# The second norm's rows turned by VectorE instead of TensorE, for two of four token blocks

## The chip, the cores and the metric

The kernel runs on one core of a Trainium2 chip. The metric is the device time of one execution in microseconds, the median of several runs. The core has five instruction streams: TensorE (matmuls, "PE" in the profile, with its weight loads as "PEld"), VectorE ("DVE"), ScalarE ("ACT"), GpSimd ("POOL") and SyncE ("SP"), which here only issues transfers. Each runs its own queue in order, and they wait for each other by semaphores.

## What is computed

One layer of a decoder for 2048 tokens of width 1024, in float32. The part that matters here is the second half:

```python
x = x + jnp.concatenate([o_hg, o_rw], axis=-1) @ w_out[l]
x = x + _conv_ffn(_rmsnorm(x, norm2_w[l]), w_up[l], conv_w[l], conv_b[l], w_down[l])
return _rmsnorm(x, final_norm_w)
```

`_rmsnorm` divides each token's row by the root of its mean square and multiplies it by a row of weights. `_conv_ffn` multiplies by `w_up` (1024 x 5632), applies a causal convolution of width 3 along the tokens, a gate with SiLU, and `w_down` (2816 x 1024).

## The kernel before

The tokens are four blocks of 512. All large products are made of three float32r matmuls: each operand is split in a high and a low part (ScalarE casts the high part, VectorE subtracts to get the low part), and high x high, high x low and low x high are summed (`mm3`, L270 to L272). The splits of weights go through rings of five buffers (`uwh`, `uwl`, L254 and L255).

Stage 1 (`phase1`) holds the first norm, the input projection, the two mixers and the output projection of blocks 0 to 2. Its constants lie in the tile `cst`. Stage 2 begins with the output projection of block 3 (L1199 to L1276), which leaves the rows of `x` after the first residual in DRAM, `x1d[b]`, one row a token.

Then comes the up-projection. It needs the normed rows with the features on the partitions: `h2d[b]`, 1024 x 512. For blocks 0 and 1 this was done in stage 1. The up-projection is written as a scheme of seven products (Strassen's, in Winograd's form) over pairs of blocks and halves of the weights: `run()` loops over `n`, 22 column blocks for blocks 0 and 1 and then 22 for blocks 2 and 3; each `n` is seven products (`prod`) of 4 x 3 matmuls of 128x512 into `ua`, `ub` and `ud`. The weights of one `n` are four loads of 256 KB (`uraw`, L1178, a ring of six), the sums of weights are L1389, L1390, L1465 and L1470, and the gated results leave as `gd`, L1497, two stores an `n`.

While blocks 0 and 1 are multiplied, the inputs for blocks 2 and 3 are prepared "aside": after each product, `aside(n)` takes one job from a list. `norm_last(b, i2)` puts in 14 jobs for each group of 256 tokens, four groups in all: a load of two tiles of 128 rows (L1298), a pause, two scalings (`rstd` on ScalarE, then L1301 on VectorE), two pauses, and eight times one step of `transposed`. A step is two transposes of 128x128 on TensorE into a PSUM bank (L264), an eviction on ScalarE that multiplies by the norm's weight of that feature, now one value a partition (L122), and a store of 128 x 256 to `h2d` (L1306). The jobs that follow in the list (`four`, L1315) read `h2d` of blocks 2 and 3 and form sums for the scheme; later ones (`sums`, L1341) form sums for the down-projection.

The tiles `h2`, the squares of `rstd` and all raw rows share one ring of six buffers, `br`. All transfers named here are issued by SP, one after the other. A scheduler that runs when the kernel is built gives the order of each engine's queue: an instruction whose inputs are there earlier can stand ahead of one that the code has before it.

The last stage is the down-projection (`da`, `db`), again seven products, with the last norm and the output.

Of the kernel before, what the change touches and what calls it, by code (L numbers as in the profile page):

```python
# [7 lines left out]
F32 = mybir.dt.float32  # L8
# [3 lines left out]
AF = mybir.ActivationFunctionType  # L12
ALU = mybir.AluOpType
# [5 lines left out]
P = 128  # L19
T = 2048  # L20
D = 1024
KD = D // P
# [45 lines left out]
def tile_layer(ctx, tc, consts, x, norm1_w, w_in, hg_lb_logits, hg_norm_w, rw_shift_mu, rw_w0, rw_w2,  # L68
# [4 lines left out]
    V, S, TE = nc.vector, nc.scalar, nc.tensor  # L73
    dma, store = nc.sync.dma_start, nc.gpsimd.dma_start
# [12 lines left out]
    cst = cp.tile([P, C_ID], F32, name="cst")  # L87
# [11 lines left out]
    def pst(name):  # L99
        return pools["ps"].tile([P, 512], F32, tag="mm", name=name, bufs=8)  # L100
# [13 lines left out]
    def act(out_, in_, func, **kw):  # L114

        want = tables.get(func)
        if want is not None and want != tab["now"]:
            pre = S.preload_act_table_set(want)
            for u_ in tab["uses"]:
                tc.add_manual_dep(pre.ins, u_.ins.name, NOSYNC, reason="table order")  # L120
            tab.update(now=want, pre=pre, uses=[])
        i_ = S.activation(out_, in_, func, **kw)  # L122
        if want is not None:
            tc.add_manual_dep(i_.ins, tab["pre"].ins.name, NOSYNC, reason="table order")
            tab["uses"].append(i_)
        return i_

    def rstd(pool, xt, name, sqt="nsq", sqb=1):

        sq = pool.tile([P, D], BF16, tag=sqt, name="nsq", bufs=sqb)  # L130
        st = pool.tile([P, 2], F32, tag="nst", name=name, bufs=8)
        act(sq, xt, AF.Square, accum_out=st[:, 0:1])
        act(st[:, 1:2], st[:, 0:1], AF.Ln, bias=eps6, scale=1.0 / D)
        act(st[:, 1:2], st[:, 1:2], AF.Exp, scale=-0.5)
        return st[:, 1:2]
# [23 lines left out]
    def vec(nm, i):  # L159
        return vt[:, off[nm] + i:off[nm] + i + 1]  # L160
# [24 lines left out]
    x1d = [dp.tile([BLK, D], F32, name=f"x1d{b}") for b in range(NBLK)]  # L185
    h2d = [dp.tile([D, BLK], F32, name=f"h2d{b}") for b in range(NBLK)]
# [71 lines left out]
    def transposed(xt, nm, psum, evict):  # L258

        n = len(xt)  # L260
        for k in range(KD):
            tp = psum()
            for i in range(n):
                TE.transpose(tp[:, i * P:(i + 1) * P], xt[i][:, k * P:(k + 1) * P], ident)  # L264
            evict(k, tp[:, :n * P], vec(nm, k))
            yield 109 * n
# [879 lines left out]
    with ExitStack() as c2:  # L1146
        wr = c2.enter_context(tc.tile_pool(name="wr2", bufs=1, reuse_waits="tile"))
        hp = c2.enter_context(tc.tile_pool(name="hp2", bufs=1, reuse_waits="tile"))
        hr = c2.enter_context(tc.tile_pool(name="hr2", bufs=1, reuse_waits="tile"))
# [33 lines left out]
        with tc.tile_pool(name="op", bufs=1, reuse_waits="tile") as op_:  # L1183
# [7 lines left out]
            b = NBLK - 1  # L1191
# [41 lines left out]
            def weights(k, dh):  # L1233
                raw = ring("w", w_out[0, k * P:(k + 1) * P, dh * 512:dh * 512 + 512])
                wh, wl = (wo_[c].pop() if wo_[c] else
                          op_.tile([P, 512], F32R, tag="wo" + c, name="wo" + c, bufs=3) for c in "hl")
                split_next(wh, wl, raw)
                return wh, wl

            xt = {}  # L1240
# [4 lines left out]
            for dh in range(2):  # L1245
                accs = [pst("wacc") for _ in range(4)]
                for n, k in enumerate((0, 1, 4, 5, 2, 3, 6, 7)):
                    w = weights(k, dh)
                    if dh == 0:
                        take(k)  # L1250
                    if n == 5:
                        for i in range(4):
                            t0 = b * BLK + i * P
# [10 lines left out]
                    if dh == 1 and 2 <= n:  # L1264
                        for j in range(2):
                            q = 2 * (n - 2) + j
# [3 lines left out]
                    for q in range(12):  # L1270
                        i, t_ = (q % 4, q // 4) if first else (q // 3, q % 3)
# [7 lines left out]
        with tc.tile_pool(name="up", bufs=1, reuse_waits="tile") as up:  # L1279
            Bh[2], Bl[2] = (hp.tile([P, 4, BLK], F32R, tag=f"B{c}2", name=f"B{c}2") for c in "hl")  # L1280
            halo = up.tile([P, 2 * NFF + 52, 2], F32, name="halo")
            V.memset(halo, 0.0)


            side, first_at = [], [1]

            def aside_of(fs):

                side.extend((first_at[0], f) for f in fs)

            def norm_last(b, i2):

                xt = []

                def load():
                    for q in range(2):
                        xt.append(up.tile([P, D], F32, tag="xt2", name="xt2", bufs=2))
                        dma(xt[q], x1d[b][(i2 * 2 + q) * P:(i2 * 2 + q + 1) * P, :])  # L1298

                def scale(q):  # L1300
                    V.tensor_scalar_mul(xt[q], xt[q], rstd(hr, xt[q], "nst", "br", 6))  # L1301

                def evict(k, tp, w):
                    t_ = hr.tile([P, 256], F32, tag="br", name="h2", bufs=6)
                    act(t_, tp, AF.Copy, scale=w)
                    dma(h2d[b][k * P:(k + 1) * P, i2 * 256:i2 * 256 + 256], t_)  # L1306

                g = transposed(xt, "n2", lambda: pst("tp"), evict)
                aside_of([load, None, lambda: scale(0), lambda: scale(1), None, None] + [lambda: next(g)] * KD)

            def four(srcs, make, dsts):

# [15 lines left out]
            for b in (2, 3):  # L1328
                for i2 in range(2):
                    norm_last(b, i2)  # L1330
# [172 lines left out]
    with tc.tile_pool(name="dn", bufs=1, reuse_waits="tile") as dn:  # L1503
# [39 lines left out]
        def evict(g, p, accs, i):  # L1543

            if p in (0, 2, 4):
                add(g, *((0, 0), None, (0, 1), None, (1, 1))[p], i, accs["a"][i])
            if p == 1:
                pend.append(lambda: add(g, 0, 0, i, accs["b"][i]))
            if p == 4:
                pend.append(lambda: add(g, 1, 1, i, accs["b"][i]))  # L1550
            if p == 5:
                pend.append(lambda: (add(g, 1, 0, i, accs["a"][i]), finish(g, 1, i)))
            if p == 6:
                pend.append(lambda: (add(g, 0, 1, i, accs["b"][i]), finish(g, 0, i)))
# [10 lines left out]
        for s_ in range(DS, N):  # L1565
            g, p, kk = steps[s_]
# [60 lines left out]
```

## Time and profile before

| | |
|---|---|
| median of 3 runs | 2648.05 us (2644.51 to 2653.97) |
| the profiled execution | 2645.14 us, its span 2643.1 us |
| mean granted clock of TensorE | 0.992 |
| TensorE busy | 2545.1 us, 96% |
| VectorE busy | 1973.0 us, 75% |
| ScalarE busy | 1356.5 us, 51% |
| GpSimd busy | 381.1 us, 14% |
| moved by the DMA engines | 523.18 MB, 198 GB/s |

The span runs from the first to the last instruction. In the views of the profile a line such as "L1306" is a line of the kernel; "out<-in" names the tiles; "xN" is a count. A group shows its busy time, the mean of one in ns, and the idle time of its engine just before, with what ended it. A window shows the busy time of each engine in it, the clock that TensorE was granted, the mean busy share of the DMA engines and what they moved. A line of waits is "engine and line <- engine and line that ended the wait: total us, times, longest". A line of one source or tile is minimum, median and maximum of the duration in ns, then the first and last start.

### The profile page before, as it was taken

To read this page: it belongs to the slowest core of one execution; us is meant where nothing else is said; L and a number is where in the kernel's file an instruction comes from. 1 tells how busy PE (TensorE), PEld (TensorE's weight loads), DVE (VectorE), ACT (ScalarE), POOL (GpSimd) and SP (SyncE) were. 2 spreads that over 40 slices of the span, in tenths; PEclk is the share of its full clock that TensorE was granted. 3 is DMA by queue.
4 is the path that set the end of the run, shared out by engine and by line. 5 is a ranking of instruction groups with operands and counts; after the bars stand their busy time and mean duration, and the time that the engine had idled before them with its cause. 6 is when DMAs were issued, how large, how long until landed. Compare 5 with 4: busy or idle time off the path is not lost. (4 is left out here: it accounts for less than half of the span.)

```text
span 2643.1 us, 51079 instructions
## 1 busy us (share of the span) xinstructions
PE 2545.1 (96%) x19403; PEld 2044.3 (77%) x19403; DVE 1973.0 (75%) x3760; ACT 1356.5 (51%) x2242; POOL 381.1 (14%) x686
## 2 busy tenths in 40 slices
PE   7999999999999899999899999999999999999998
PEld 5877777767777667777678888787888887888887
DVE  4978576676676765787678799987998887766556
ACT  5565444555445554354466754556554544545444
POOL 6433222212222122232100000000000000000000
PEclk9999999999999999999999999999999999999999
DMA  8847464656665566856574477747764553998665
GB/s 305 243 161 204 141 173 128 149 152 212 191 180 145 168 212 184 262 167 164 188 260 136 129 233 255 230 152 228 245 204 130 169 172 128 337 318 280 204 192 187
DMA packets 415115, 523.18 MB, mean 198 GB/s; under 512 B 149280, under 2 KB 245910, under 8 KB 414870
## 3 DMA queue, kind: packets, MB, share of 16 engines
q1 hardware_dynamic: 360337, 341.59, 41.3%
q0 software_dynamic: 54464, 178.32, 21.1%
q8 instruction: 152, 2.49, 0.4%
q14 instruction: 94, 0.76, 0.1%
q10 hardware_dynamic: 68, 0.02, 0.0%
HBM read 372.99 MB, written 134.22 MB: 192 GB/s over the span
## 5 line engine op out<-in xcount | busy, mean ns | idle before, releaser
L270 PE MATMUL pj<-hh,wh 128*128 128x512 f32 x960 | 392.3, 409 | 4.7 <-ACT rkv L122 2.1
L271 PE MATMUL pj<-hl,wh 128*128 128x512 f32 x960 | 379.1, 395 | 0.0
L272 PE MATMUL pj<-hh,wl 128*128 128x512 f32 x960 | 378.3, 394 | 0.0
L270 PE MATMUL ua<-Bh,uwh 128*128 128x512 f32 x704 | 276.9, 393 | 6.7 <-ACT m L122 5.8
L272 PE MATMUL ua<-Bh,uwl 128*128 128x512 f32 x704 | 274.5, 390 | 0.0
L271 PE MATMUL ua<-Bl,uwh 128*128 128x512 f32 x704 | 274.3, 390 | 0.0
L270 PEld LDWEIGHTS pj<-hh,wh 128*128 128x128 f32 x960 | 181.2, 189 | 53.7 <-issue 9.0
L272 PEld LDWEIGHTS pj<-hh,wl 128*128 128x128 f32 x960 | 181.3, 189 | 39.3 <-issue 0.3
L271 PEld LDWEIGHTS pj<-hl,wh 128*128 128x128 f32 x960 | 181.5, 189 | 35.1 <-issue 0.6
L254 ACT CAST uwh<-uraw 128x512 fp32r<-128x512 f32 x220 | 134.1, 617 | 128.7 <-PE ua L271 54.1
L255 DVE TENSOR_TENSOR dal<-draw,dah 128x512 fp32r<-128x512 f32 x138 | 95.4, 691 | 107.0 <-ACT dah L254 106.7
L255 DVE TENSOR_TENSOR uwl<-uraw,uwh 128x512 fp32r<-128x512 f32 x220 | 147.6, 687 | 33.7 <-ACT uwh L254 33.6
L254 ACT CAST dah<-draw 128x512 fp32r<-128x512 f32 x138 | 85.6, 621 | 159.2 <-PE da L271 74.0
L270 PEld LDWEIGHTS ua<-Bh,uwh 128*128 128x128 f32 x704 | 132.2, 188 | 38.3 <-ACT m L122 10.6
L272 PEld LDWEIGHTS ua<-Bh,uwl 128*128 128x128 f32 x704 | 132.2, 188 | 28.0 <-DVE uwl L255 0.4
L271 PEld LDWEIGHTS ua<-Bl,uwh 128*128 128x128 f32 x704 | 132.3, 188 | 26.7
L270 PE MATMUL ud<-Bh,uwh 128*128 128x512 f32 x352 | 138.1, 392 | 0.0
L1497 POOL DMA_DIRECT2D gd<-y x2 | 1.1, 540 | 947.9 <-DVE y L1495 947.9
L272 PE MATMUL ud<-Bh,uwl 128*128 128x512 f32 x352 | 137.2, 390 | 0.0
L271 PE MATMUL ud<-Bl,uwh 128*128 128x512 f32 x352 | 137.1, 390 | 0.0
L271 PE MATMUL da<-dbl,dah 128*128 128x512 f32 x332 | 129.5, 390 | 0.2 <-DVE dbl L255 0.2
L272 PE MATMUL da<-dbh,dal 128*128 128x512 f32 x332 | 129.3, 389 | 0.0
(581 smaller groups left out, 6191.6 us busy)
## 6 DMA issues: line engine op xcount, KB each, us to landing
uraw<-in_w_up_dram SPq DMA_DIRECT2D x176, 256.0 KB
woraw<-in_w_out_dram POOLq DMA_DIRECT2D x96, 256.0 KB, 3.4
br<-gd SPq DMA_DIRECT2D x88, 256.0 KB
draw<-Sg SPq DMA_DIRECT2D x88, 256.0 KB
draw<-Tw SPq DMA_DIRECT2D x88, 256.0 KB
gd<-y SPq DMA_DIRECT2D x86, 256.0 KB
Sg<-br SPq DMA_DIRECT2D x72, 256.0 KB
xt<-x1d SPq DMA_DIRECT2D x32, 512.0 KB
```

The costliest lines, as they stand in the source:

```text
L254: S.copy(hi, src)
L255: V.tensor_sub(lo, src, hi.bitcast(F32))
L270: TE.matmul(acc, lh, rh, start=first, stop=False, skip_group_check=skip)
L271: TE.matmul(acc, lh, rl, start=False, stop=False, skip_group_check=skip)
L272: TE.matmul(acc, ll, rh, start=False, stop=last, skip_group_check=skip)
L1497: (dma if end is None else nc.gpsimd.dma_start)(gd_[2 * h + b][fb * P:(fb + 1) * P, :], ys[0][:, b * BLK:(b + 1) * BLK])
```

## The change

The eight steps of each `norm_last` group become four "turns" with a pause after each, so the list of jobs keeps its length. VectorE transposes each 32x32 block on its own, so that a block's 32 tokens lie along the free dimension and its 32 features on 32 partitions; the rest of the transposition is in the addresses of the stores. The 256 tokens of a group are loaded so that each quarter of the partitions holds 64 tokens in a row, as two sets of 32 (four loads of 256 KB for two of 512 KB). One turn takes 256 features: one instruction of 128 x 512 elements and four stores, each from 32 partitions, 64 KB in runs of 256 bytes.

The norm's weight is no longer one value a partition at that point. It is multiplied in the scaling, with a row of weights that is the same on all partitions: `n2row`, loaded once, 512 KB, over the first 1024 columns of `cst`, which stage 2 doesn't use.

```diff
             V.memset(halo, 0.0)
+            n2row = cst[:, 0:D]
+            dma(n2row, norm2_w.broadcast_to([P, D]))
...
                 def load():
-                    for q in range(2):
-                        xt.append(up.tile([P, D], F32, tag="xt2", name="xt2", bufs=2))
-                        dma(xt[q], x1d[b][(i2 * 2 + q) * P:(i2 * 2 + q + 1) * P, :])
+                    xt.append(up.tile([P, 2, D], F32, tag="xt2", name="xt2"))
+                    v = x1d[b][i2 * 256:i2 * 256 + 256, :].rearrange("(g q t) d -> g t q d", g=4, q=2)
+                    for g in range(4):
+                        dma(xt[0][32 * g:32 * g + 32], v[g])
 
                 def scale(q):
-                    V.tensor_scalar_mul(xt[q], xt[q], rstd(hr, xt[q], "nst", "br", 6))
-
-                def evict(k, tp, w):
-                    t_ = hr.tile([P, 256], F32, tag="br", name="h2", bufs=6)
-                    act(t_, tp, AF.Copy, scale=w)
-                    dma(h2d[b][k * P:(k + 1) * P, i2 * 256:i2 * 256 + 256], t_)
-
-                g = transposed(xt, "n2", lambda: pst("tp"), evict)
-                aside_of([load, None, lambda: scale(0), lambda: scale(1), None, None] + [lambda: next(g)] * KD)
+                    t_ = xt[0][:, q]
+                    V.scalar_tensor_tensor(t_, t_, rstd(hr, t_, "nst", "br", 6), n2row, ALU.mult, ALU.mult)
+
+                def turn(m):
+                    t_ = hr.tile([P, 8, 2, 32], F32, tag="br", name="h2", bufs=6)
+                    V.transpose(t_.rearrange("p c q t -> p q c t"),
+                                xt[0][:, :, m * 256:m * 256 + 256].rearrange("p q (c t) -> p q c t", t=32))
+                    for g in range(4):
+                        t0 = i2 * 256 + g * 64
+                        dma(h2d[b][m * 256:m * 256 + 256, t0:t0 + 64].rearrange("(c p) t -> p c t", p=32),
+                            t_[32 * g:32 * g + 32].rearrange("p c q t -> p c (q t)"))
+
+                aside_of([load, None, lambda: scale(0), lambda: scale(1), None, None]
+                         + [f for m in range(4) for f in (lambda m=m: turn(m), None)])
```

## The prediction

> **What bounds the kernel now.** I read the page first, then the stage of the change in windows, then its waits.
>
> ```profile
> span 2643.1 us, 51079 instructions
> PE 2545.1 (96%) x19403; PEld 2044.3 (77%) x19403; DVE 1973.0 (75%) x3760; ACT 1356.5 (51%) x2242; POOL 381.1 (14%) x686
> ```
>
> TensorE is busy 96% of the span, so the question is whether it is also what sets the pace where the transposes stand. I cut the second stage at the first `ub` matmul of a pass of the up-projection (one pass is 7 products, 84 matmuls). The first row holds the eight passes in which the norm is done, the second the next five, the third the five after those; the last two are single passes of the first eight.
>
> ```profile
> 1378.80:1539.30 160.50, 160.50 (x737) 131.62 (x736) 126.46 (x194) 109.95 (x182) 0.00 (x0) 1.00 0.40 127
> 1539.30:1634.50 95.20, 95.20 (x422) 78.83 (x421) 92.38 (x145) 47.70 (x70) 0.00 (x0) 1.00 0.80 264
> 1634.50:1733.80 99.30, 96.45 (x423) 78.60 (x422) 91.41 (x147) 48.48 (x72) 0.00 (x0) 1.00 0.72 234
> ...
> 1499.20:1518.70 19.50, 19.50 (x90) 16.06 (x89) 16.56 (x26) 15.54 (x26) 0.00 (x0) 1.00 0.38 126
> 1518.70:1539.30 20.60, 20.60 (x99) 16.87 (x97) 14.89 (x24) 12.16 (x21) 0.00 (x0) 1.00 0.44 136
> ```
>
> Columns: length, then busy time of PE, PEld, DVE, ACT, POOL, granted clock, DMA share, GB/s. In the norm passes TensorE is busy for all of 160.50 us, at full clock, and a pass is longer the more transposes it holds (4 in the 19.50, 12 in the 20.60). The next five passes have none and take 95.20/5 = 19.04 us each, TensorE again without a gap although VectorE is at 92.38/95.20 = 97%. In the third row TensorE does lose 99.30 - 96.45 = 2.85 us. Who waits in the norm passes:
>
> ```profile
> ACT uwh L254 <- PE ua L271: 30.0, 20, 2.0
> DVE uwl L255 <- ACT uwh L254: 20.6, 16, 2.3
> ```
>
> ScalarE waits 30 us for TensorE to give a weight buffer back, and VectorE waits for ScalarE: the makers of the operands run as far ahead as their five buffers allow. TensorE itself is missing from the list of waits here. So this stage is TensorE's, and its own instructions are what counts.
>
> **What is removed.** 64 transposes in 32 pairs, 32 evictions on ScalarE, 32 stores of 128 KB.
>
> ```profile
> L264 PEld LDWEIGHTS tp<-ident,xt x64: 138/139/144, 1395.0 to 1536.4; 128*128 128x128 f32 x64
> L264 PE MATMUL tp<-ident,xt x64: 270/271/275, 1395.2 to 1536.5; 128*128 128x128 f32 x64
> L122 ACT ACTIVATE h<-tp,vt x32: 467/468/472, 1395.7 to 1536.9; 128x256 f32<-128x256 f32 x32
> ```
>
> 64 times 271 ns would be 17.3 us, but matmuls overlap, so the price is read from the starts:
>
> ```profile
> 1394.77 0.39 PE L271 MATMUL ua<-Bl,uwh 128*128 128x512 f32 x1
> 1394.99 0.39 PE L272 MATMUL ua<-Bh,uwl 128*128 128x512 f32 x1
> 1395.22 0.38 PE L264 MATMUL tp<-ident,xt 128*128 128x128 f32 x2
> 1395.36 0.47 PE L270 MATMUL ud<-Bh,uwh 128*128 128x512 f32 x1
> 1395.67 0.39 PE L271 MATMUL ud<-Bl,uwh 128*128 128x512 f32 x1
> ```
>
> From 1394.99 to 1395.67 there are two steps of 0.23 and the pair: 0.68 - 0.46 = 0.22 us a pair, 32 x 0.22 = 7.0 us. The windows give more: 160.50 - 8 x 19.04 = 8.2 us. I take 8.2, since it is the whole difference between passes with and without, and keep 7.0 as the low end. ScalarE loses 15.0 us of evictions; it was waiting there already, so I count nothing.
>
> **What is added to VectorE.** Four turns a group, 16 in all, each 128x512, and the two scalings of a group become a scaling with a row of weights.
>
> ```profile
> L765 DVE STREAM_TRANSPOSE ATb<-AR 128x512 f32<-128x512 f32 x16 | 10.9, 694 | 0.0
> L810 DVE STREAM_TRANSPOSE TZ<-Ti 128x512 f32<-128x512 f32 x8 | 8.5, 1061 | 0.8 <-DMA xt<-in_x_dram 0.2
> L1301 DVE TENSOR_SCALAR xt<-xt,nst 128x1024 f32<-128x1024 f32 x8 | 5.7, 751 | 0.2
> L1490 DVE SCALAR_TENSOR_TENSOR y<-cg,cvt,y 128x1024 f32<-128x1024 f32 x44 | 56.2, 1278 | 0.0
> ```
>
> L765 reads whole runs, L810 reads with a stride. The new turn reads runs of 256 elements and scatters whole 32-element rows, so it is nearest to L765: 16 x 0.694 = 11.1 us (17.0 by L810). The scaling: 8 x (1.278 - 0.751) = 4.2 us. VectorE then has 126.5 + 15.3 = 141.8 us in 8 x 19.04 = 152.3, 93% (97% by L810). The fullest passes are those with two scalings and a turn: 16.56 + 0.69 + 1.05 = 18.3 of 19.04. The five passes of the second row ran at 97% without a loss, so I charge nothing inside the stage. What hides it is the lead; after it come those five passes, which may live on it. If they arrive without it they could lose as the third row does, 2.85/99.3 x 95.2 = 2.7 us. Between 0 and 2.7 I take 0.8, since VectorE still idles 10 us in the stage.
>
> [...]
>
> **What is added to SP's queue.** 64 stores of 64 KB in runs of 256 B instead of 32 of 128 KB in runs of 1 KB, and four loads a group for two.
>
> ```profile
> L1306 SPq DMA_DIRECT2D h2d<-h x32: 319/320/413, 1396.2 to 1537.4; - x32
> L757 SPq DMA_DIRECT2D KBT<-KBb x128: 591/640/3207, 89.0 to 1201.6; - x128
> L1298 SPq DMA_DIRECT2D xt<-x1d x8: 319/376/752, 1367.9 to 1497.7; - x8
> L1178 SPq DMA_DIRECT2D uraw<-in_w_up_dram x172: 367/384/1269, 1365.8 to 2208.7; - x172
> ...
> 716.66 11.37 SPq L757 DMA_DIRECT2D KBT<-KBb  x11
> ...
> 709.74 1.96 SPq L745 DMA_DIRECT2D Ed<-M  x4
> 715.46 1.15 SPq L748 DMA_DIRECT2D E<-Ed  x2
> ```
>
> The nearest issue is L757, 64 KB from 32 partitions in short runs: 0.64 us, or 11.37/11 = 1.03 us each in a row. In one group, two passes of 38.1 us, SP issues 16 such stores, 4 loads, 8 weight loads and 4 stores of the gate: 16 x 0.69 + 16 x 0.45 = 18.2 us with the gaps, 23.7 us at 1.03. SP has room. Behind a store that waits for its turn on VectorE stand the weight loads, and behind those ScalarE's cast. Their slack:
>
> ```profile
> 1436.77 0.39 SPq L1178 DMA_DIRECT2D uraw<-in_w_up_dram  x1
> ...
> 1445.99 0.69 DVE L1389 TENSOR_TENSOR s<-uraw 128x512 f32<-128x512 f32 x1
> ```
>
> 9.2 us from issue to first use, against 4 x 1.03 = 4.1 us for the four stores of a turn. I charge 0. The first row of windows has the DMA engines at 0.40, so bytes are not short either. The reads of the second norm's rows by the next job wait for the same distance of jobs as before, so nothing moves there.
>
> **The row of weights.** One load of 4 KB to each of 128 partitions, 512 KB, into the space of the constants, which have their last reader at 1267.6 us. It has no wait left; where it stands in SP's queue the trace cannot show.
>
> ```profile
> L1006 DVE COPY_PREDICATED A<-cst,hg x80: 217/227/302, 108.8 to 1267.6; 128x64 f32<-128x64 uint32 x80
> ...
> 1300.00:1310.00 10.00, 8.81 (x34) 5.82 (x34) 9.34 (x13) 9.36 (x15) 2.36 (x4) 1.00 0.15 49
> ...
> 1365.00:1370.00 5.00, 3.28 (x14) 2.18 (x12) 4.20 (x8) 4.13 (x8) 0.00 (x0) 1.00 0.88 274
> ...
> 1355.42 2.11 SPq L1276 DMA_DIRECT2D x1d<-xh  x4
> 1357.62 2.74 SPq L1161 DMA_DIRECT2D br<-Ts  x4
> ...
> 1363.36 2.61 ACT L247 CAST Bh<-br 128x512 fp32r<-128x512 f32 x4 [4.33 <-DMA br<-Ts]
> ```
>
> In the code it stands behind the stores L1276. There ScalarE waits 4.33 us for the loads of `Ts`, and TensorE has 3.28 of 5 us: whatever delays those loads is paid by TensorE. 512 KB at 274 GB/s are 1.9 us, and with an issue of 0.38 it is 2.3 us. But SP's queue is not in the order of the code (the loads of L1161 run past L1276), and with no wait the load can slip into a hole such as 1300 to 1310, where the DMA share is 0.15: then it costs 0. I take 1.0.
>
> **The sum.** -8.2 + 0.8 + 0 + 1.0 = -6.4 us against the profiled execution, 2645.14 us (a span of 2643.1 and 2.0 around it): 2638.7. The median of the runs is 2648.05, 2.9 above that execution, so the forecast for the median is 2641.6.
>
> **Rivals.**
>
> *VectorE becomes the bound.* For it: 18.3 of 19.04 us in the fullest passes, in-order behind ScalarE, and 97% if a turn costs what L810 does. Against it: the second row. If the norm passes lose at the third row's rate, 2.9% of 152.3 = 4.4 us, and the next five 2.7: -8.2 + 4.4 + 2.7 + 1.0 = -0.1, 2648.
>
> *The small stores hold SP up (the other side).* Place: SP's queue in the norm passes. The stage is then 4 x (16x + 7.2) us for x us a store. It overtakes TensorE's 38.1 us a group from x = 1.93 and the old stage from x = 2.06. For it: L757 has one of 3.207 us, and four stores to DRAM (Ed, runs of 128 B) had landed only within 715.46 - 709.74 = 5.7 us, 1.43 each. Against it: that is under 1.93, and those stretches carried other traffic; with one row of many for it I give it 0.10. Halfway between 1.43 and 3.2, x = 2.3: 4 x 44.0 = 176.0, +15.5 and 1.0 for the row: 2664.5. [...]
>
> *More is gained.* ScalarE has 15 us less and operands arrive earlier; if the 2.85 us of the third row go too and the row slips into a hole: -8.2 - 2.85 = -11.0, 2637. Against it: VectorE, not ScalarE, is late in that row.
>
> *The change does nothing for the pace.* Only if something else than TensorE paced the norm passes; it has no idle time there, so this gets no chance of its own.
>
> **How the numbers follow.** Forecast 0.60, VectorE's bound 0.16, slow stores 0.10, more gained 0.14. The forecast's own bounds are -8.2 and -7.0 + 2.3 + 2.7 = -2.0, so 2639.9 to 2646.0. The range takes in -11 and the spread of the runs shown (2644.51 to 2653.97, -3.5 and +5.9 around the median): 2635 to 2652. It leaves out the slow stores and a few odd runs. A measurement tells about 0.3%, 7.9 us, from no change. Faster by more: nearly all of the last case and a quarter of the forecast (its lower edge, with the spread), 0.29; slower: the slow stores and a little of VectorE's bound, 0.12; within: 0.59.
>
> **What would show it.** Right: no `tp` matmuls, passes of 19.04 us from the first norm pass on, TensorE without waits there, the turn near 0.69 us and the scaling near 1.28. VectorE's bound: TensorE idle behind `uwl` or behind `m` between 1380 and 1634. Slow stores: issues of `h2d` above 1.9 us and ScalarE waiting for `uraw`. The row: TensorE's hole at 1365 to 1370 grows by up to 2.3 us. I am wrong if the norm passes are at 19.04 and the end does not come earlier: then the later stages gave it back.

## The result, and the profile after

The changed kernel is slower: 2681.53 us median (2676.73 to 2685.71, 4 runs) beside 2648.11 us (2644.51 to 2653.97) for the kernel before on the same chip, a ratio of 1.0123 with a 95% interval of 1.0098 to 1.0149. Forecast were 2641.6 us and a range of 2635 to 2652. All ratios here are to the kernel before on the same chip; one execution of 7472.41 us, in the longer repetition with GpSimd's stores, stands outside its ratio.

The page of the changed kernel, its head and the busy times:

```profile
span 2678.6 us, 50886 instructions
...
PE 2557.1 (95%) x19339; PEld 2049.3 (77%) x19339; DVE 1985.7 (74%) x3776; ACT 1345.2 (50%) x2210; POOL 381.1 (14%) x686
```

TensorE has 64 matmuls fewer and is nevertheless busy for 12.0 us more, and the span has grown by 35.5 us. VectorE has 12.7 us more work, ScalarE 11.3 us less. So the totals show that something went wrong, but not where. The windows do. Here are single passes of the up-projection in the changed kernel, cut at the first `ub` matmul of each (length, then busy time of PE, PEld, DVE, ACT, POOL, granted clock, DMA share, GB/s); the last row is nine passes together.

```profile
1396.90:1415.90 19.00, 19.00 (x85) 15.74 (x84) 11.74 (x19) 8.23 (x11) 0.00 (x0) 1.00 0.47 122
1415.90:1451.00 35.10, 25.79 (x86) 18.94 (x85) 22.80 (x35) 15.87 (x27) 0.00 (x0) 0.81 0.31 80
1451.00:1470.00 19.00, 19.00 (x85) 15.60 (x84) 11.44 (x18) 8.47 (x12) 0.00 (x0) 1.00 0.48 128
1470.00:1500.70 30.70, 23.64 (x86) 17.30 (x85) 22.43 (x34) 15.23 (x26) 0.00 (x0) 0.89 0.33 88
1500.70:1519.70 19.00, 19.00 (x86) 15.62 (x84) 12.10 (x20) 9.16 (x13) 0.00 (x0) 1.00 0.49 132
1519.70:1550.60 30.90, 23.42 (x86) 17.57 (x85) 23.08 (x35) 15.74 (x26) 0.00 (x0) 0.89 0.36 94
1550.60:1569.60 19.00, 19.00 (x85) 15.61 (x84) 11.58 (x19) 8.68 (x13) 0.00 (x0) 1.00 0.43 129
1569.60:1597.10 27.50, 22.93 (x86) 17.90 (x85) 23.89 (x39) 11.22 (x17) 0.00 (x0) 0.88 0.60 202
...
1376.30:1597.10 220.80, 191.12 (x757) 149.98 (x757) 158.50 (x239) 107.43 (x167) 0.00 (x0) 0.92 0.41 116
```

The same nine passes of the kernel before:

```profile
1378.80:1558.40 179.60, 179.60 (x821) 147.42 (x820) 145.56 (x224) 119.88 (x197) 0.00 (x0) 1.00 0.44 142
```

Every second pass from 1396.90 on is the 19.04 us of the forecast (19.00 in windows cut to a tenth). Between them stand four long passes: 35.10, 30.70, 30.90 and 27.50 us. The first three hold the squares of the second to the fourth group of 256 tokens. The pass with the squares of the first group, from 1376.30, takes 20.60 us, and the fourth long pass holds no squares. Nine passes take 220.80 us in place of 179.60, that is 41.2 more. The stage starts 2.5 us earlier than before and what follows it is 3.2 us shorter (2678.6 - 1597.1 = 1081.5 against 2643.1 - 1558.4 = 1084.7), which leaves the 35.5 us of the span.

The 220.80 us are made of three parts. Nine passes at 19.04 are 171.4. TensorE is idle for 220.80 - 191.12 = 29.7. The rest, 191.12 - 171.4 = 19.7, is the same matmuls taking longer, most of it, by an estimate, by the clock: in the long passes the granted clock is 0.81 to 0.89, and length times what it lacks of 1.00, idle time included, adds up to 16.8 us in the four (6.7, 3.4, 3.4 and 3.3). At a clock of 0.50, around 1427, the matmuls start 0.43 us apart, at 1.00, around 1417, 0.23. The first long pass in small windows, and the matmuls that follow a wait in it:

```profile
1419.00:1423.70 4.70, 0.00 (x0) 0.00 (x0) 4.70 (x7) 1.56 (x2) 0.00 (x0) 0.89 0.00 0
1423.70:1426.00 2.30, 2.12 (x4) 1.31 (x5) 2.29 (x4) 2.28 (x3) 0.00 (x0) 0.50 0.30 111
1426.00:1428.00 2.00, 2.00 (x6) 1.52 (x6) 1.03 (x3) 0.15 (x1) 0.00 (x0) 0.50 0.98 277
...
1430.00:1432.00 2.00, 2.00 (x10) 1.68 (x9) 0.00 (x0) 0.33 (x1) 0.00 (x0) 1.00 0.27 77
...
1435.00:1438.80 3.80, 0.15 (x1) 0.00 (x0) 1.34 (x4) 3.61 (x10) 0.00 (x0) 1.00 0.00 0
...
1442.00:1446.00 4.00, 4.00 (x11) 3.04 (x10) 4.00 (x8) 0.00 (x0) 0.00 (x0) 0.50 0.61 147
```

```profile
1423.75 0.79 PE L270 MATMUL ua<-Bh,uwh 128*128 128x512 f32 x1 [4.90 <-ACT uwh L254]
...
1438.88 0.50 PE L270 MATMUL ua<-Bh,uwh 128*128 128x512 f32 x1 [3.73 <-ACT uwh L254]
```

After 4.90 us without a matmul the clock is 0.50, and the first matmul takes 0.79 us where one of the kernel before takes 0.39; the window from 1430 is back at 1.00. Behind the hole of 3.73 us the first matmul still takes 0.50 us, and the clock falls a little later: 0.50 in the window from 1442. So the holes are paid about one and two thirds times: 29.7 + 19.7 = 49.4 us for 29.7. In the first case the clock is still 0.50 at 1428, 4.3 us after the matmuls start again, and 1.00 from 1430, after 6.3 us. The length of a hole alone doesn't decide here: behind a hole of 2.54 us that ended at 1473.29 the clock is 0.50 from 1473.90 to 1477.30, and behind another of 2.54 us that ended at 1523.01 it is 1.00 up to 1528.

Who waits, in the nine passes of the changed kernel:

```profile
ACT m L122 <- PE ua L272: 57.3, 19, 4.9
...
PEld ua L270 <- ACT uwh L254: 22.7, 10, 5.3
PE ua L270 <- ACT uwh L254: 18.7, 7, 4.9
```

In the kernel before, ScalarE waited 30.0 us for TensorE to give weight buffers back. Now TensorE waits mostly for ScalarE's cast (18.7 us; another 9.1 us for VectorE's split `uwl`), and ScalarE at the same time waits 57.3 us for TensorE's products: each stands at something that the other will only do later. ScalarE's queue shows how that is possible. First the changed kernel in the first long pass, then the kernel before in the same place (start, duration, then in brackets the idle time before and what ended it):

```profile
1422.13 1.06 ACT L122 ACTIVATE y<-y 128x1024 f32<-128x1024 f32 x1 [3.60 <-DVE y L1498]
1423.09 0.60 ACT L254 CAST uwh<-s 128x512 fp32r<-128x512 f32 x1
...
1429.73 0.60 ACT L122 ACTIVATE m<-ua 128x512 f32<-128x512 f32 x1 [3.58 <-PE ua L272]
1435.19 0.60 ACT L122 ACTIVATE m<-ua 128x512 f32<-128x512 f32 x1 [4.86 <-PE ua L272]
1435.69 1.05 ACT L122 ACTIVATE nsq<-xt 128x1024 bf16<-128x1024 f32 x1
...
1438.23 0.60 ACT L254 CAST uwh<-uraw 128x512 fp32r<-128x512 f32 x1
```

```profile
1430.53 0.60 ACT L122 ACTIVATE m<-ua 128x512 f32<-128x512 f32 x1
1431.29 0.62 ACT L254 CAST uwh<-s 128x512 fp32r<-128x512 f32 x1 [0.16 <-DVE s L1390]
1432.62 0.62 ACT L254 CAST uwh<-s 128x512 fp32r<-128x512 f32 x1 [0.70 <-PE ua L271]
1433.15 0.59 ACT L122 ACTIVATE m<-ua 128x512 f32<-128x512 f32 x1
```

In the kernel before, casts stand between the evictions (`m`), so the next weights are made while TensorE works. In the changed kernel two evictions, two squares (`nsq`) and their root stand in a row, with the cast that TensorE needs next behind them; the cast starts as soon as they are through, without a wait of its own. That is the second hole. The first is less plain: the cast at 1423.09 stands behind a gate function that waited 3.60 us for VectorE, but the sum `s` that it casts was itself only just made, because on VectorE too it stood behind work of the gate:

```profile
1422.01 0.69 DVE L1398 TENSOR_TENSOR s<-s,uraw 128x512 f32<-128x512 f32 x1
```

So this trace alone doesn't tell whether ScalarE's order or VectorE's makes the first hole; the kernel before with only ScalarE's order exchanged, further down, does.

This order is fixed when the kernel is built. Written as letters (C a weight cast, m an eviction of `ua`, v an eviction into `cv`, y a gate function, N a square, t the small steps behind it, h an eviction of transposes), two passes of ScalarE's queue read:

```
before   mytttCtmCCmChvyChyChChymChChmChmChvyCNyNCC
changed  mymmvyCyyCCCmNNtttmtCCCCmCvCyCCyCC
```

`mm`, `yy` and `NN` now stand together, and the casts in lumps. The change touches none of the casts, evictions and gate functions, and takes the h out. A pass needs seven casts; the number of casts that stand ahead of a pass's third eviction, beyond seven for each pass already over, is the lead that the order allows. Read off the built orders of the kernels of this study, passes 2 to 7:

```
kernel before                              9 10  9 10  9 10
changed kernel                             8  9  5  8  5  8
changed, stores from GpSimd                8  9  8  9  9  9
changed, stores of 128 partitions          8  9  8  9  8  9
changed, natural order, GpSimd             9  9  9  9  9  9
changed, SP's order held                   8  9  5  9  5  9
before, loads of 32 partitions             8 10  9  9  9  9
before, row of weights                     9 10  9 10  9 10
```

(Some of the expectations below count the casts beyond eight a pass; for passes 2 to 7 their figures are smaller than these by 1 to 6.) In the changed kernel the lead is 5 in passes 4 and 6, the first two long ones, and in pass 8, the third. The fourth long pass has a lead of 9. Its holes, 2.54 us behind `uwl` and 2.03 us behind `uwh`, come ahead of its first eviction, and this measure doesn't see them. VectorE's order moved as well: where each pass of the kernel before makes two sums of weights, passes 3, 5, 7 and 9 of the changed kernel make none and the passes behind them four. VectorE's order was not held by itself in any run.

### The profile page after: what moved, and what is told of

Same layout as the page of the kernel before. It is cut to its first block, busy times and chain, and to the rows that moved or that the text cites. A ratio compares the mean times of both kernels' runs of the same rounds, so it can differ in the third digit from the quotient of the medians.

```text
span 2678.6 us, 50886 instructions
## 1 busy us (share of the span) xinstructions
PE 2557.1 (95%) x19339; PEld 2049.3 (77%) x19339; DVE 1985.7 (74%) x3776; ACT 1345.2 (50%) x2210; POOL 381.1 (14%) x686
## 4 chain that ended last, share of the span: by engine, by line
PE 63%; issue 11%; DVE 8%; DMA 7%; ACT 7%; POOL 3%; SPq 0%; DVEq 0%; POOLq 0%; ACTq 0%
PE pj L270 6%; PE pj L271 5%; PE pj L272 5%; PE ua L272 5%; PE ua L270 5%; PE ua L271 5%; PE da L271 3%; PE da L272 3%; PE da L270 3%; PE ud L270 2%; PE ud L271 2%; PE ud L272 2%; PE db L272 2%; PE db L270 2%; PE db L271 2%
## 5 line engine op out<-in xcount | busy, mean ns | idle before, releaser
L255 DVE TENSOR_TENSOR dal<-draw,dah 128x512 fp32r<-128x512 f32 x138 | 95.3, 691 | 111.4 <-ACT dah L254 108.1
L1505 POOL DMA_DIRECT2D gd<-y x2 | 1.1, 540 | 983.7 <-DVE y L1503 983.7
```

The source lines that it names most:

```text
L255: V.tensor_sub(lo, src, hi.bitcast(F32))
L1505: (dma if end is None else nc.gpsimd.dma_start)(gd_[2 * h + b][fb * P:(fb + 1) * P, :], ys[0][:, b * BLK:(b + 1) * BLK])
```

## The experiments

The theory to be tested (A): the loss is ScalarE's and SP's queue order alone, not the time of any instruction that the change brings. Its rivals: the 64 small stores hold SP up by their own time (B), or VectorE's turns and scalings make the splits late (C). Orders were held by dependencies that set a place in the queue but wait for nothing; the other queues were then free to be scheduled anew around them. The expectations of the first four runs (the two with ScalarE's order alone, the first with GpSimd's stores, and the row of weights) were written before the letters were settled; each says itself what it sets against what.

**Only the order, without the change.** The kernel before, with its transposes and its stores, and ScalarE's queue held to the order of the changed kernel.

```diff
+    def keep_order():
+        of = lambda w: seen[w.split(".")[0]][int(w.split(".")[1])]
+        for a, b in zip(ACT_ORDER, ACT_ORDER[1:]):
+            tc.add_manual_dep(of(b).ins, of(a).ins.name, NOSYNC, reason="order on ScalarE")
...
-        S.copy(hi, src)
+        note("C" if name == "uw" else "-", S.copy(hi, src))
...
-                            act(m, acc, AF.Copy)
+                            note(tag, act(m, acc, AF.Copy))
```

> The kernel before, with its TensorE transposes and wide stores; only ScalarE's queue is held, over the norm passes, to the order that the changed kernel has. Theory order: long passes appear without any turn or small store, about four of 27 to 35 us, time 2675 to 2695. Theories stores and VectorE: no small store and no turn is here, so about 2648.

Measured: 2683.59 us (2682.22 to 2688.71), 1.0149 of the kernel before (1.0122 to 1.0175). Its nine passes, and who waited on TensorE:

```profile
1377.20:1597.70 220.50, 194.83 (x821) 153.05 (x820) 147.15 (x224) 118.49 (x199) 0.00 (x0) 0.95 0.38 121
```

```profile
PE ua L282 <- ACT uwh L266: 12.3, 7, 4.4
PE ub L284 <- DVE uwl L267: 7.6, 3, 2.5
```

220.50 us, where the changed kernel has 220.80, with the same wait for the cast at the head. No turn, no small store and no row of weights is in this kernel. ScalarE's order, with what the scheduler places around it, makes a loss as large as that of the change. It also settles the first hole. Here VectorE makes the sum early, in the pass before, and its cast still comes 16.6 us after the sum is done, behind a gate function, and TensorE waits 4.40 us for it:

```profile
1408.40 0.69 DVE L1402 TENSOR_TENSOR s<-s,uraw 128x512 f32<-128x512 f32 x1
...
1425.68 0.60 ACT L266 CAST uwh<-s 128x512 fp32r<-128x512 f32 x1
```

**The change, with ScalarE's order of before.** The same mechanism in the changed kernel, with the list of the kernel before.

```diff
+        for a, b in zip(ACT_ORDER, ACT_ORDER[1:]):
+            tc.add_manual_dep(of(b).ins, of(a).ins.name, NOSYNC, reason="order on ScalarE")
```

> The changed kernel, all of its instructions and transfers kept; only ScalarE's queue is held, over the norm passes, to the order that the kernel before has (casts, evictions, gates, squares). Theory order (the casts of the weights now stand behind evictions that wait for TensorE, so they no longer run ahead): the passes return to 19.04 us, no long pass of 27 to 35 us is left, time 2638 to 2646. Theory stores (64 stores in runs of 256 B hold up SP and the weights arrive late): nothing changes, about 2681. Theory VectorE (turns and scalings make VectorE the bound): nothing changes, about 2681.

Measured: 2659.26 us (2647.47 to 2670.18), 1.0042 (1.0022 to 1.0061). Two thirds of the loss is gone and a third stays; the 2638 to 2646 us expected were missed. Nine passes, the waits, and SP's own:

```profile
1375.00:1571.00 196.00, 180.57 (x758) 144.22 (x757) 158.32 (x239) 108.85 (x171) 0.00 (x0) 0.97 0.50 133
```

```profile
ACT uwh L266 <- DVE s L1410: 35.0, 5, 9.0
DVE s L1409 <- DMA uraw<-in_w_up_dram: 18.4, 4, 5.2
```

```profile
SPq L1190 <- DVE uwl L267: 46.2, 9, 11.0
SPq L1517 <- DVE y L1515: 42.4, 9, 10.2
```

Now the casts wait for sums of weights (`s`), these for raw weights, and on SP the gate's stores (L1517, L1497 in the kernel before) wait 42.4 us for VectorE, with weight loads behind them. In the kernel before, that wait was 8.8 us, and in the changed kernel (L1505) 95.3 us:

```profile
SPq L1497 <- DVE y L1495: 8.8, 9, 1.3
...
SPq L1505 <- DVE y L1503: 95.3, 9, 12.4
```

So SP's order was disturbed too. Whether it is that, or the stores' own time on SP, the next run tells.

**Both orders held.** As above, and SP's weight loads and gate stores in the order of the kernel before. The 64 stores stay on SP, the turns on VectorE.

```diff
+        for a, b in zip(SP_ORDER, SP_ORDER[1:]):
+            tc.add_manual_dep(of(b).ins, of(a).ins.name, NOSYNC, reason="order on SyncE")
```

> The changed kernel with two queues held to the order of the kernel before: ScalarE's casts, evictions, squares and gate functions, and SP's weight loads and gate stores. Its 64 stores stay on SP, its turns on VectorE. Theory A (the loss is the order alone, and what x_order still lost, 11 us, is SP's weight loads behind gate stores that wait): the norm passes fall to 19.04 to 20 us and the time to 2636 to 2646. Theory B (the stores' own time on SP delays the weight loads): the 11 us stay, 2655 to 2662. Theory C (VectorE's turns and scalings hold the splits up): they stay too, and TensorE's waits name VectorE's split.

Measured: 2644.41 us (2640.61 to 2652.43), 1.0000 (0.9982 to 1.0019). The whole loss is gone:

```profile
1375.00:1553.00 178.00, 173.84 (x758) 141.19 (x757) 158.72 (x239) 108.25 (x171) 0.00 (x0) 1.00 0.52 145
```

Full clock, SP's wait for the gate down to 4.6 us, and 178.0 us with the same stores on the same queue and the same work on VectorE (158.72 us busy, 158.50 in the changed kernel). B and C fall as causes of the loss. Yet the time isn't below that of the kernel before, although the transposes are gone; on that, see the next section.

**SP's order alone.** The loop over `ACT_ORDER` taken out again; the edit is shown against the kernel with both orders held.

```diff
-        for a, b in zip(ACT_ORDER, ACT_ORDER[1:]):
-            tc.add_manual_dep(of(b).ins, of(a).ins.name, NOSYNC, reason="order on ScalarE")
```

> The changed kernel with SP's order of weight loads and gate stores held to that of the kernel before, and ScalarE's queue left free. Its built order keeps the changed kernel's lead of casts: 7, 7, 2, 5, 0, 3 ahead of the third eviction of passes 2 to 7. Theory A (ScalarE's order decides, SP's adds to it only once ScalarE's is mended): one long pass per group stays, 2668 to 2684. Theory B (SP's order alone would do): about 2644, as xs_order.

Measured: 2680.29 us (2674.93 to 2683.37), 1.0131 (1.0108 to 1.0153). The time is as A had it: with ScalarE's lead still at 5 in every other pass, SP's order brings nothing. The picture isn't. The long passes are not one per group here: from 1418.80 on each of the next four takes 24.1 to 28.3 us, and TensorE waits as long for VectorE's split (13.3 us) as for ScalarE's cast (12.9).

```profile
1379.20:1595.90 216.70, 186.82 (x757) 148.79 (x756) 156.66 (x234) 106.40 (x165) 0.00 (x0) 0.92 0.43 114
```

The four cases together:

| ratio to the kernel before | SP as in the changed kernel | SP's order of before |
|---|---|---|
| ScalarE as in the changed kernel | 1.0123 (1.0098 to 1.0149) | 1.0131 (1.0108 to 1.0153) |
| ScalarE's order of before | 1.0042 (1.0022 to 1.0061) | 1.0000 (0.9982 to 1.0019) |

**Which part of the change moves the order.** Three edits, without any order held. First, GpSimd issues the 64 stores:

```diff
-                        dma(h2d[b][m * 256:m * 256 + 256, t0:t0 + 64].rearrange("(c p) t -> p c t", p=32),
+                        store(h2d[b][m * 256:m * 256 + 256, t0:t0 + 64].rearrange("(c p) t -> p c t", p=32),
```

> The changed kernel with the 64 stores issued by GpSimd instead of SP. Theory order: the order of the casts depends on what stands in SP's queue; here most casts are back ahead of the evictions, but the squares of every other group still stand late, so 2641 to 2655. Theory stores: SP is free of them, but if it is their landing that is slow the reads of the normed rows come late; 2640 if only the issue is slow, 2660 and more if the landing is. Theory VectorE: about 2681, the turns are all there.

> The kernel of c_pool again with more repetitions: the changed kernel with its 64 stores issued by GpSimd. c_pool gave 0.9979 [0.9961, 0.9998] of the kernel before. If the removed transposes (8.2 us of TensorE's passes) less two passes of 20.6 us in place of 19.04 (3.1 us) are what is left, 5 us of 2648, the ratio comes out near 0.998 and its interval stays under 1. If c_pool's lead was scatter, the ratio comes nearer to 1.

Measured: 2639.77 us (2635.28 to 2649.78), 0.9979 (0.9961 to 0.9998), and in the longer repetition 2641.0 us, 0.9990 (0.9976 to 1.0003). The loss is gone without holding anything. Of a gain the second, tighter run leaves no more than 0.24%, and it can't tell it from none. Nine passes and the stores of the repetition:

```profile
1379.80:1555.50 175.70, 172.92 (x758) 141.56 (x757) 159.34 (x240) 108.03 (x166) 36.98 (x64) 1.00 0.54 153
```

```profile
L1313 POOL DMA_DIRECT2D h2d<-h x64: 585/585/618, 1395.4 to 1520.5; - x64
```

Second, SP keeps the stores but they leave from 128 partitions, two a turn, rows stored where they lie:

```diff
-                    for g in range(4):
-                        t0 = i2 * 256 + g * 64
-                        dma(h2d[b][m * 256:m * 256 + 256, t0:t0 + 64].rearrange("(c p) t -> p c t", p=32),
-                            t_[32 * g:32 * g + 32].rearrange("p c q t -> p c (q t)"))
+                    for r in range(2):
+                        dma(h2d[b][m * 256 + r * P:m * 256 + r * P + P, i2 * 256:i2 * 256 + 256],
+                            t_.rearrange("p c q t -> p (c q t)")[:, r * 256:r * 256 + 256])
```

> The changed kernel with each turned pair of blocks stored by two transfers of 128 partitions (256 KB) in place of four of 32; the rows are stored where they lie, so the stored values stand in another order than the reference's and the output differs. VectorE's work, the four-piece loads and SP as the issuer stay. ScalarE's built order keeps its casts ahead: 7, 7, 5, 5, 3, 3 ahead of the third eviction of passes 2 to 7. Theory A (order): the long passes are gone, 2636 to 2650. Theory C (VectorE's turns cost): VectorE's work is that of the changed kernel, so 2655 or more.

Measured: 2638.17 us (2632.83 to 2642.66), 0.9975 (0.9958 to 0.9992). That is 0.25% below the kernel before, with an interval that ends just under 1, as that of the first run with GpSimd's stores did; it was not repeated.

```profile
1380.30:1556.90 176.60, 172.71 (x757) 141.58 (x756) 160.45 (x242) 108.02 (x167) 0.00 (x0) 1.00 0.53 155
```

VectorE's work is all there, 160.45 us, and the long passes are not: C falls a second time. Third, the kernel before with only the loads in four pieces of 32 partitions:

```diff
-                    for q in range(2):
-                        xt.append(up.tile([P, D], F32, tag="xt2", name="xt2", bufs=2))
-                        dma(xt[q], x1d[b][(i2 * 2 + q) * P:(i2 * 2 + q + 1) * P, :])
+                    t_ = up.tile([P, 2, D], F32, tag="xt2", name="xt2")
+                    xt.extend(t_[:, q] for q in range(2))
+                    v = x1d[b][i2 * 256:i2 * 256 + 256, :].rearrange("(q p) d -> p q d", q=2)
+                    for g in range(4):
+                        dma(t_[32 * g:32 * g + 32], v[32 * g:32 * g + 32])
```

> The kernel before with its loads of 128 token rows replaced by the changed kernel's four loads of 32 partitions for a turn's 256 rows; everything else as before, transposes included. ScalarE's built order has 7, 8, 6, 5, 4, 3 casts ahead of the third eviction of passes 2 to 7, so Theory A (order) expects no long pass: 2640 to 2655, within 0.3% of before. If narrow loads cost by themselves, SP's four issues and a late square would show: 2655 or more.

Measured: 2646.16 us (2642.31 to 2653.66), 1.0004 (0.9990 to 1.0019). The loads aren't it. So it is the 64 stores from 32 partitions on SP's queue that bring the scheduler to the bad order: with them the lead is 5 in every other pass, without them 8 or more, and the times go with it. The wide stores are also half as many and twice as large, so whether their number, their size or their partitions counts isn't separated. Why the scheduler answers to them so was not taken apart; no run here shows it.

**Other parts.** The row of weights alone, in the kernel before:

```diff
+            n2row = cst[:, 0:D]
+            dma(n2row, norm2_w.broadcast_to([P, D]))
...
-                    V.tensor_scalar_mul(xt[q], xt[q], rstd(hr, xt[q], "nst", "br", 6))
+                    V.scalar_tensor_tensor(xt[q], xt[q], rstd(hr, xt[q], "nst", "br", 6), n2row, ALU.mult, ALU.mult)
...
-                    act(t_, tp, AF.Copy, scale=w)
+                    act(t_, tp, AF.Copy)
```

> The kernel before with the row of weights alone: the norm's weight is multiplied in the scaling (two operands, 1.28 us for 0.75) and the eviction multiplies by nothing; transposes, loads and stores as before. All theories: 2647 to 2651, the scalings lie in VectorE's idle time and the row's load stands in a hole. Theory VectorE would take anything above 2652 as a first sign.

Measured: 2642.43 us (2634.52 to 2649.52), 0.9985 (0.9970 to 1.0000), below the range expected. It costs nothing.

Twice as many stores of half the size, with the tokens in natural order, two wide loads, GpSimd issuing:

```diff
-                    v = x1d[b][i2 * 256:i2 * 256 + 256, :].rearrange("(g q t) d -> g t q d", g=4, q=2)
-                    for g in range(4):
-                        dma(xt[0][32 * g:32 * g + 32], v[g])
+                    for q in range(2):
+                        dma(xt[0][:, q], x1d[b][(i2 * 2 + q) * P:(i2 * 2 + q + 1) * P, :])
...
+                        t0 = i2 * 256 + g * 32
+                        for q in range(2):
+                            store(h2d[b][m * 256:m * 256 + 256, t0 + q * P:t0 + q * P + 32].rearrange("(c p) t -> p c t", p=32),
+                                t_[32 * g:32 * g + 32, :, q])
```

> The blocks turned with the tokens in their natural order, so that two loads of 128 partitions do as before, and 128 stores of 32 KB, twice as many at half the size, issued by GpSimd. ScalarE's built order has 8, 7, 6, 5, 4, 3 casts more than eight per pass done ahead of the third eviction of passes 2 to 7 (before 8, 8, 6, 6, 4, 4; the changed kernel 7, 7, 2, 4, 0, 2). Theory A (the order decides): 2634 to 2646. Theory B (narrow stores cost by themselves): twice the stores, norm passes above 20.6 us, 2648 or more.

Measured: 2641.26 us (2634.69 to 2649.24), 0.9989 (0.9969 to 1.0009): pieces of 128 B do no harm to the time either.

Last, both orders of before held, and the stores on GpSimd.

```diff
+        for a, b in zip(ACT_ORDER, ACT_ORDER[1:]):
+            tc.add_manual_dep(of(b).ins, of(a).ins.name, NOSYNC, reason="order on ScalarE")
+        for a, b in zip(SP_ORDER, SP_ORDER[1:]):
+            tc.add_manual_dep(of(b).ins, of(a).ins.name, NOSYNC, reason="order on SyncE")
...
-                        dma(h2d[b][m * 256:m * 256 + 256, t0:t0 + 64].rearrange("(c p) t -> p c t", p=32),
+                        store(h2d[b][m * 256:m * 256 + 256, t0:t0 + 64].rearrange("(c p) t -> p c t", p=32),
```

> The same two orders held, and the 64 stores issued by GpSimd as in c_pool. Theory A: what c_pool still lost, two passes of 20.58 us, is order too and goes: all norm passes 19.04, time 2633 to 2640, that is 1 to 4 us below c_pool's 2639.77. Theory B or C: the order gives nothing more, 2638 to 2642, and the passes of 20.58 stay.

Measured: 2642.81 us (2641.10 to 2648.63), 0.9994 (0.9977 to 1.0010). A's number here was a miss: holding the order of the kernel before gains nothing over GpSimd's stores alone (0.9979 and 0.9990). The ratios can't tell these runs apart. In the profiled executions the nine passes take 178.70 us here and 175.70 there, so the order of the kernel before doesn't look like the best one for the changed kernel.

```profile
1377.50:1556.20 178.70, 174.63 (x757) 140.77 (x757) 158.33 (x238) 108.83 (x171) 36.98 (x64) 1.00 0.49 145
```

## Why the prediction was wrong

Step by step, in the prediction's order.

*The bound.* Right for the kernel before. The step that failed is the sentence drawn from it: "the makers of the operands run as far ahead as their five buffers allow". It was taken as a property of the buffers, and it is one of the queue's order as well: the makers run ahead only as far as their instructions stand ahead. In the changed kernel the lead of casts falls to 5 in three of the long passes (9 in the kernel before), TensorE waits 18.7 us for casts, and the nine passes take 220.80 us where nine at the forecast 19.04 would be 171.4; with both orders of before held they take 178.0. The reading of 30.0 us of `uwh` waiting for `ua` was true for the order that stood there, and the change came with another. The same failure is in "I charge 0" for SP, where the slack of 9.2 us was measured in the old order.

*That the order could change* was said, but used only for one load ("SP's queue is not in the order of the code"). None of the rivals has ScalarE's queue as its place. The rival on the slower side had SP's small stores, 2664.5 us; the direction fits and the mechanism doesn't, since with the orders held the same stores cost nothing that can be measured (1.0000 from SP, 0.9994 from GpSimd).

*The removed transposes, -8.2 us.* In the windows of the changed kernel the other passes are at the forecast 19.04 us. But with the orders of before, nine passes go from 179.6 to 178.0, not to 171.4. There TensorE is idle for 178.00 - 173.84 = 4.2 us, and its waits name evictions and splits alike:

```profile
PE ua L285 <- ACT m L122: 2.3, 6, 0.5
PE ua L287 <- DVE uwl L270: 1.9, 2, 1.0
```

With the wide stores and with GpSimd's stores, in the orders that the scheduler gave them, the nine passes gain 3.0 and 3.9 us (176.6 and 175.7). With the wide stores five of them take 19.0 to 19.1 us and four, those with the squares, 20.3 to 20.5, each with one wait of about 1 us (3.9 us in all) for an eviction; the first is 1.11 us and ends at 1389.76. So the price of the transposes is right where no such wait stands, and the term was mis-sized as a whole, by more than half: the sum took passes without any wait, and every order tried without the transposes brought waits of its own. Whether some order would give the whole 8.2 us, no run shows.

*The turns, the scaling, the stores, the row.* The prices of the instructions were right, or too high. In the changed kernel:

```profile
L1309 DVE STREAM_TRANSPOSE h<-xt x16: 700/705/715, 1391.1 to 1550.3; 128x512 f32<-128x512 f32 x16
```

```profile
L1305 DVE SCALAR_TENSOR_TENSOR xt<-xt,nst,cst x8: 1277/1284/1285, 1386.3 to 1539.6; 128x1024 f32<-128x1024 f32 x8
```

```profile
L1313 SPq DMA_DIRECT2D h2d<-h x64: 332/462/1299, 1391.8 to 1565.4; - x64
```

```profile
L1284 SPq DMA_DIRECT2D cst<-in_norm_w_dram x1: 424/424/424, 1274.6 to 1274.6; - x1
```

A turn is 0.705 us (0.694 charged), a scaling 1.284 (1.278), a store's issue 0.462 (0.64 to 1.03 thought), and the load of the row is issued at 1274.6. That isn't the hole that the prediction named: the DMA engines are 0.75 busy between 1270 and 1280. It costs nothing all the same, as the low end had it (0.9985 for the kernel before with the row alone). The 16 turns took 16 x 0.705 = 11.3 us (11.1 charged). That VectorE's work is hidden was right: with 158.72 us of it in 178.0 the time is that of the kernel before.

*The small runs.* The stores go from runs of 1 KB to runs of 256 B, and the measurements show no effect on the time here: 1.0000 with 64 such stores on SP, 0.9989 with 128 stores in pieces of 128 B from GpSimd. GpSimd's 64 stores landed 2.0 to 4.9 us after their issue, 3.2 in the median, in the longer repetition. How long SP's took to land isn't shown.

*The signs named at the end.* "TensorE idle behind `uwl` or behind `m`" was to mean that VectorE is the bound. TensorE is idle behind `uwl`, but mostly behind `uwh`; the sign was read off the engine that ended the wait, and the kernel before with only ScalarE's order exchanged shows the same sign without any turn. A list of waits names who came last, not why it came late.

What stays open: why the scheduler, given stores from 32 partitions, lumps casts and evictions, and how the loss divides among the queues, VectorE's among them, as each held order lets the scheduler place the rest anew.

## What to carry to other kernels

When a scheduler places the queues at build time, a change of some transfers can reorder engines that it doesn't touch; compare the order of each in-order queue before and after, above all how far the producers stand ahead of the consumers, before adding up instruction times. Slack measured in a trace belongs to the order that the trace had. If a change loses more than its instructions can explain, hold the old order in the new kernel and the new order in the old one: that separates the change from its schedule. Here it took two queues: ScalarE's old order alone left a third of the loss.

## What was not expected

The holes on TensorE cost more than themselves: the clock was 0.50 behind those of 4.90 and 3.73 us and behind one of two of 2.54 us, and 29.7 us of holes came with 19.7 us of slower matmuls. A turn, which reads runs of 256 elements and scatters 32-element rows, took 0.705 us, no more than 2% above the turn of whole runs (0.694). A store of 64 KB from 32 partitions in runs of 256 B took 0.462 us to issue on SP and 0.585 on GpSimd (medians), and GpSimd, with nothing else to do there, took all 64 (36.98 us) without a trace in the time.
